# Moving a 32-block operator build from GpSimd to VectorE, and eight operator blocks of the next layer to another stage, in a two-layer SSD, GLA and S5 backbone

## The chip, the core and the metric

The kernel runs on one core of a Trainium2 chip. The metric is the device time of one execution in microseconds (us). The core has five engines that each work through their own list of instructions in order: TensorE (PE, matrix products into PSUM), VectorE (DVE), ScalarE (ACT), GpSimd (POOL) and SyncE (SP), which in this kernel issues every DMA.

## The reference, cut to what matters

A hidden stream `h` of 1024 channels by 768 tokens (256 context tokens, then 512 latent ones) passes through two layers. A layer is

```
u = rmsnorm(h) * (1 + scale) + shift
p = u @ in_proj                                  # z, x, B, C, dt | q, k, v, gates | S5 input and gate
y_ssd = ssd(...)   y_gla = gla(...)   y_s5 = s5(...)    # each in both directions, context first
h = h + gate * (concat(y_ssd * norm, y_gla, y_s5) @ out_proj)
```

The S5 branch is a linear recurrence `h_t = lam_bar * h_{t-1} + bu_t` with a complex diagonal `lam_bar`, a complex input matrix B and an output matrix C, for 32 groups of 16 channels with 64 states. The kernel does it in chunks of 8 tokens. For that it builds, per layer, from the powers of `lam_bar`:

- input operators: powers times B, in 8 blocks of 128x1024 (`s5_in_map`); they bring the 8 tokens of a chunk to the chunk's state;
- output operators: powers times C, in 16 blocks of two groups (`s5_out_map`); they bring a chunk's starting state to its 8 outputs, and with a small matrix product they give the part inside the chunk.

None of them depends on the tokens.

## The kernel before

All matrix operands are split into a high and a low part, and each product is three passes (`PASSES`): high by high, low by high, high by low. The input projection, the S5, GLA and SSD branches, their norms and the output projection are written one after another in `layer(l, u)`. A tile framework's scheduler then sorts the instructions of each engine by its own timeline of the whole program, so the order on an engine is not that of the text. SBUF tiles come from pools with tags: "cs" has 3 buffers of 128x1024, "bc" 2, "cv" 3, "bA" and "bB" one large buffer each (128x6144), "m" is one more, and "hl" has 8 for split operands. Who wants a buffer waits until its last reader is done.

The steps that the prediction speaks of:

- `s5_lambda(l)` makes the powers of `lam_bar` (tile `pw`) and writes the operands of the input operators to DRAM (`lpD`). For layer 1 it also runs in layer 0, since the ACT tables and inputs are there.
- `s5_in_map(l, bi)`, L351 to L363: loads `bb` (256 KB, L353) and `lp` (512 KB, L354), then six DVE instructions of 128x512: two products at L360, two at L361, a sum or difference at L363, twice over. The blocks of layer 0 stay in SBUF (`bls`, in bB and bA). Those of layer 1 are built in layer 0, in bA ahead of the projection of the S5 inputs, stored to `blD` (L580, 512 KB each) and loaded again in layer 1 (L602, two buffers in turn).
- `s5_out_map(l, bi, pw, buf)`, L365 to L404: loads `cb` (L370); GpSimd negates a 128x32 piece (L375) and makes the two halves of the operator in six instructions of 128x288 (L380 to L385); the result goes to DRAM (`clD`, L388); 16 small matrix products (L394) make the part inside the chunk from it, ACT copies it (L121), VectorE corrects its diagonal (L400, L401), and it goes to DRAM (`gD`). Both layers' calls run in layer 0, 16 ahead of the S5 scan and 16 behind it.
- L608 applies the input operators; L643 to L646 are the scan over chunks on VectorE; L688 and L689 apply the output operators.
- SSD ends with the sums at L928 (into `xy`); L968 multiplies by the gate, which comes from `zD`; L974, L981 and L438 make the norm, and L421 splits the normed tiles to bA and bB. The S5 outputs pass a gated unit (L1026, L1037, L1039) and are split at L421 to "hl", as are the GLA outputs that are loaded from `ygD` (L1047).
- `spilled_part` is the first half of the output projection: eight column blocks of matrix products (L1062, L1064) over the S5 and GLA operands in "hl", each added to `h` by VectorE (L1075, L1076) and stored (`hpD`). The second half takes the SSD operands in bA and bB.

```
yss = ssd_norm(0) + ssd_norm(1)
spilled_part(h1D if last else hT, 8, [a[:, :, t0:NT] for a in ygl + ys5], (4, 5, 6, 7, 0, 1, 2, 3))
```

`dma` is `nc.sync.dma_start` everywhere, so one queue holds all loads and stores in the scheduler's order. Where an entry waits for a buffer or a result, the entries behind it wait too.

Of the kernel before, what the change touches and what calls it, by code (L numbers as in the profile page):

```python
# [41 lines left out]
def hybrid_backbone_kernel(  # L42
# [52 lines left out]
    def m12():  # L95
        return T("m12", [128, 3072], 1)
# [90 lines left out]
    h1D = dram([1024, LL], "h1D")  # L187
    lpD = [dram([512, 128], f"lpD{l}") for l in range(2)]
    pwD = dram([128, 704], "pwD1")
    blD = dram([8, 128, 1024], "blD1")  # L190
    clD = [dram([16, 128, 512], f"clD{l}") for l in range(2)]
# [159 lines left out]
    def s5_in_map(l, bi, lp, bb, tb, bl):  # L351
# [6 lines left out]
        for o in range(2):  # L358
# [4 lines left out]
            V.tensor_tensor(blo, blo, tb, SUB if o == 0 else ADD)  # L363

    def s5_out_map(l, bi, pw, buf):  # L365

        gs = 2 * bi
        w5, tmp, cb, cn = cuts(buf, 576, 288, 128, 32)
        gt = tmp[:, 0:240]
# [4 lines left out]
        t54 = tmp.rearrange("p (g k h) -> p g k h", g=2, k=9)  # L374
        G.tensor_scalar(cn, cb[:, 0:32], -1.0, None, MUL)  # L375
        shp = [128, 2, 9, 16]
        pr, pi = (pw[:, :, a, gs : gs + 2].rearrange("p k g -> p g k").unsqueeze(3).to_broadcast(shp) for a in range(2))
        cr, ci, cm = (x.rearrange("p (g h) -> p g h", g=2).unsqueeze(2).to_broadcast(shp)
                      for x in (cb[:, 0:32], cb[:, 32:64], cn))
        G.tensor_tensor(w54[:, 0], pr, cr, MUL)  # L380
        G.tensor_tensor(t54, pi, ci, MUL)
        G.tensor_tensor(w54[:, 0], w54[:, 0], t54, SUB)  # L382
        G.tensor_tensor(w54[:, 1], pi, cm, MUL)
        G.tensor_tensor(t54, pr, ci, MUL)
        G.tensor_tensor(w54[:, 1], w54[:, 1], t54, SUB)  # L385
        for d in range(2):
# [89 lines left out]
    def layer(l, u):  # L476
# [93 lines left out]

        wa = wa0 if not last else big("bA")
        if not last:
            sv, wk, lt, tw, tu, pwl = cuts(wa, 480, 512, 512, 576, 576, 704)
            s5_lambda(1, sv, wk, lt, tw, tu, pwl[:, 0:576], pwl[:, 576:704])
            dma(pwD, pwl)
            for bi in range(8):
                lp = wa[:, 1024 * (bi % 2) : 1024 * (bi % 2) + 1024]
                bb, tb, bl = cuts(wa[:, 2048:4096], 512, 512, 1024)
                s5_in_map(1, bi, lp, bb, tb, bl)
                dma(blD[bi], bl)  # L580
        for i in range(4):
# [16 lines left out]
        for bi in range(16):  # L598
            if bi % 2 == 0:
                blt = bls[bi // 2] if not last else wa[:, 4096 + 1024 * (bi // 2 % 2) : 5120 + 1024 * (bi // 2 % 2)]  # L600
                if last:
                    dma(blt, blD[bi // 2])  # L602
            bl = blt.rearrange("p (a g x) -> p a g x", a=2, g=4)[:, :, 2 * (bi % 2) : 2 * (bi % 2) + 2, :]
            pst = (px, ps)[bi % 2](384)
            for gg in range(2):
                for a in range(2):
                    o = (gg * 2 + a) * 96
                    PE.matmul(pst[:, o : o + 96], bl[:, a, gg, :], ug(2 * bi + gg), start=True, stop=True)  # L608
            pv = pst.rearrange("p (g r i) -> p i r g", g=2, r=2)
            gsl = slice(2 * bi, 2 * bi + 2)  # L610
            act(st[0:64, :, :, gsl], pv[0:64], AF.Copy)
            V.tensor_copy(st[64:128, 0:32, :, gsl], pv[64:128, 31::-1])
            V.tensor_copy(st[64:128, 32:96, :, gsl], pv[64:128, 95:31:-1])
# [52 lines left out]
        hn = hn.rearrange("p r c g -> p r g c")  # L666
        if not last:
            pw1 = T("s5p", [128, 576], 1)
            dma(pw1, pwD[:, 0:576])
        c0 = 32 if last else 0  # L670
# [406 lines left out]

        def spilled_part(src, k0, rhs, order):
            for m in range(8):
                p_c, p_l = out_part(m, k0, rhs, order)  # L1080
                ho = cv(NT)
                dma(ho[:, t0:NT], src[128 * m : 128 * m + 128])
                residual(ho, ho, m, p_c, p_l)
                dma(hpD[l][128 * m : 128 * m + 128, t0:NT], ho[:, t0:NT])

        yss = ssd_norm(0) + ssd_norm(1)
# [11 lines left out]
        for m in range(8):  # L1098
# [13 lines left out]
            if m == 6:  # L1112

                act(ho[:, 0:1] if last else T("l8", [128, 128], 1)[:, 0:1], acc[:, 0:1], AF.Ln, scale=0.0, bias=1.0)
        return hx2, (acc, sq)
# [34 lines left out]
    t = [bct(), bct()]  # L1150
    wa0, wb0 = big("bA"), big("bB")
    bls = [wb0[:, 1024 * i : 1024 * i + 1024] for i in range(6)] + [wa0[:, 4096 + 1024 * i : 5120 + 1024 * i] for i in range(2)]
    lps, bbs = [a[:, 0:1024] for a in t], [a[:, 1024:1536] for a in t]
    for bi in range(8):
        s5_in_map(0, bi, lps[bi % 2], bbs[bi % 2], wa0[:, 3360:3872], bls[bi])
    hx, acc = layer(0, u)
# [7 lines left out]
    rsqrt_rows(nrm[:, 0:NT])  # L1164
    u = norm_in(1, hx, nrm)
    hx, acc = layer(1, u)
    pr = pa()
# [92 lines left out]
```

## Time and profile before

| | |
|---|---|
| median of 3 runs | 1699.73 us (1698.31 to 1706.64) |
| profiled execution | 1712.97 us |
| its span, first to last instruction | 1711.3 us, mean granted TensorE clock 0.901 |
| PE busy | 1418.1 us, 83% |
| VectorE busy | 1168.2 us, 68% |
| GpSimd busy | 783.2 us, 46% |
| ScalarE busy | 679.9 us, 40% |
| moved by DMA | 243.55 MB, 142 GB/s over the span |

The profile is of one execution, which was 13.2 us longer than the median. Busy time is the time in which an engine had an instruction running; a stretch of the program can be held by an engine that is idle half of the span elsewhere. So the shares of the span say little, and the stages are looked at one by one. In layer 0 they are: input operators and the first projections (to about 300 us), the S5 scan and the first outputs (to 465), the second set of output operators with GLA and the convolution (to 700), SSD (to 868), the norms (to 885), and the output projection (to 1022). Layer 1 runs its S5 scan from 1119 to 1230 us and ends at 1711.

### The profile page before, as it was taken

What the parts mean: (1) busy time and instruction counts of PE and PEld (TensorE: products, weight loads), DVE (VectorE), ACT (ScalarE), POOL (GpSimd) and SP (SyncE); (2) the same over time, 40 slices, a digit from 0 to 9 for tenths busy, and PEclk for the clock granted to TensorE, in tenths of its full rate; (3) what the DMA queues carried; (4) which work ended last, traced back from release to release, by engine and by line L of the source; (5) the groups of instructions that cost most, each with busy time, mean ns of one, the idle gap of its engine ahead of it and who ended that gap; (6) DMA issues with size and microseconds to landing.
All of it is one profiled execution on the core that took longest, in us unless ns stands there. A gap on an engine that the chain in (4) does not pass through costs nothing.

```text
span 1711.3 us, 23539 instructions
## 1 busy us (share of the span) xinstructions
PE 1418.1 (83%) x8536; PEld 1145.2 (67%) x8536; DVE 1168.2 (68%) x1992; ACT 679.9 (40%) x1220; POOL 783.2 (46%) x716
## 2 busy tenths in 40 slices
PE   3867766888989779977779999997889989967886
PEld 2656655777966557755668786886678777745665
DVE  7977558995477567679994127289835986688752
ACT  4312223225342336646553124343345345545442
POOL 3615647632268843445463141164123323656454
PEclk9788987898988889988889999998988999988998
DMA  8474654332543354444455745522363242344542
GB/s 308 124 185 135 178 150 135 93 118 71 176 123 86 100 165 140 142 154 139 128 187 188 282 135 178 189 85 80 111 193 107 64 139 93 119 138 145 184 131 96
DMA packets 139885, 243.55 MB, mean 142 GB/s; under 512 B 31992, under 2 KB 72568, under 8 KB 139768
## 3 DMA queue, kind: packets, MB, share of 16 engines
q1 hardware_dynamic: 139768, 242.04, 45.3%
q8 instruction: 67, 1.10, 0.3%
q14 instruction: 50, 0.41, 0.1%
HBM read 192.81 MB, written 49.18 MB: 141 GB/s over the span
## 4 chain that ended last, share of the span: by engine, by line
PE 25%; DVE 18%; DMA 13%; POOL 6%; issue 4%; ACT 4%; SPq 0%; DVEq 0%; ACTq 0%; POOLq 0%
PE pl L492 7%; PE pl L1062 6%; DMA bA<-acsD 5%; DMA bB<-acsD 3%; PE pc L494 2%; PE pc L1064 2%; DVE xy L863 1%; DMA wr<-in_wblk 1%; ACT bA L121 1%; POOL wl L416 1%; DVE bB L916 1%; DVE bA L916 1%; DVE xy L645 1%; DMA cs<-zD 1%; DVE bA L644 1%
## 5 line engine op out<-in xcount | busy, mean ns | idle before, releaser
L492 PE MATMUL pl<-hl,wh 128*128 128x512 f32 (+1 forms) x1184 | 411.5, 414 | 15.9 <-DVE ev L511 12.3
L416 POOL TENSOR_TENSOR wl<-wr,wh 128x1024 fp32r<-128x1024 f32 (+1 forms) x82 | 210.4, 2566 | 308.5 <-ACT wh L121 284.6
L492 PEld LDWEIGHTS pl<-hl,wh 128*128 128x128 f32 (+1 forms) x1184 | 226.0, 195 | 73.5 <-DVE ev L511 13.6
L492 PE MATMUL pl<-hl,wl 128*128 128x512 f32 (+1 forms) x592 | 243.5, 412 | 20.0 <-POOL wl L416 10.7
L121 ACT ACTIVATE wh<-wr 128x1024 fp32r<-128x1024 f32 (+1 forms) x122 | 127.6, 1047 | 283.7 <-PE pc L1064 69.3
L494 PE MATMUL pc<-hl,wh 128*128 128x256 f32 (+1 forms) x864 | 202.0, 304 | 11.3 <-DVE ev L511 7.2
L494 PEld LDWEIGHTS pc<-hl,wh 128*128 128x128 f32 (+1 forms) x864 | 152.5, 202 | 26.1 <-DVE ev L511 8.7
L492 PEld LDWEIGHTS pl<-hl,wl 128*128 128x128 f32 (+1 forms) x592 | 115.4, 195 | 49.1 <-POOL wl L416 12.0
L494 PE MATMUL pc<-hl,wl 128*128 128x256 f32 (+1 forms) x432 | 128.6, 298 | 0.0
L1062 PE MATMUL pl<-hl,wh 128*128 128x512 f32 x256 | 87.7, 419 | 16.9 <-ACT hl L121 4.6
L394 PE MATMUL pa<-cs 64*32 64x128 f32 x512 | 42.9, 305 | 64.0 <-POOL cs L382 27.3
L494 PEld LDWEIGHTS pc<-hl,wl 128*128 128x128 f32 (+1 forms) x432 | 87.3, 202 | 2.7 <-issue 1.7
L121 ACT ACTIVATE ev<-pl 128x512 f32<-128x512 f32 (+1 forms) x96 | 51.1, 534 | 87.7 <-PE pl L709 43.9
L709 PE MATMUL pl<-wh,hl 128*128 128x256 f32 x384 | 79.6, 307 | 2.6 <-ACT ev L121 2.6
L416 DVE TENSOR_TENSOR wl<-wr,wh 128x1024 fp32r<-128x1024 f32 x40 | 55.4, 1386 | 38.3 <-ACT wh L121 38.1
L121 ACT ACTIVATE bB<-bB 128x512 f32<-128x512 f32 (+4 forms) x40 | 45.7, 1142 | 85.1 <-DMA bB<-acsD 52.3
L394 PEld LDWEIGHTS pa<-cs 64*32 64x32 f32 x512 | 21.5, 115 | 80.6 <-POOL cs L382 28.9
L863 DVE SCALAR_TENSOR_TENSOR xy<-ev,par_sb,xy 128x512 f32<-128x512 f32 (+1 forms) x112 | 74.8, 704 | 0.6
L375 POOL TENSOR_SCALAR cs<-cs 128x32 f32<-128x32 f32 x32 | 20.1, 629 | 118.4 <-DMA cs<-in_s5cb 43.3
L709 PEld LDWEIGHTS pl<-wh,hl 128*128 128x128 f32 x384 | 66.9, 214 | 7.8 <-ACT ev L121 3.8
L1062 PEld LDWEIGHTS pl<-hl,wh 128*128 128x128 f32 x256 | 49.8, 199 | 31.1 <-ACT hl L121 6.7
L709 PE MATMUL pl<-wl,hl 128*128 128x256 f32 x192 | 58.4, 308 | 3.8 <-DVE wl L416 3.8
(483 smaller groups left out, 3604.4 us busy)
## 6 DMA issues: line engine op xcount, KB each, us to landing
wr<-in_wblk SPq DMA_DIRECT2D x80, 512.0 KB
wr<-in_wout SPq DMA_DIRECT2D x32, 512.0 KB
hl<-in_mod_w SPq DMA_DIRECT2D x20, 512.0 KB
bA<-acsD SPq DMA_DIRECT2D x10, 1024.0 KB
bB<-acsD SPq DMA_DIRECT2D x10, 1024.0 KB
clD<-cs SPq DMA_DIRECT2D x64, 128.0 KB
cs<-clD SPq DMA_DIRECT2D x32, 256.0 KB
cs<-in_mod_w SPq DMA_DIRECT2D x16, 512.0 KB
```

The costliest lines, as they stand in the source:

```text
L121: return S.activation(out, in_, f, **kw)
L375: G.tensor_scalar(cn, cb[:, 0:32], -1.0, None, MUL)
L394: PE.matmul(pk[d][32 * gg : 32 * gg + 32], b0[64 * d : 64 * d + 64, a, :], w54[64 * d : 64 * d + 64, a, gg, d : 8 + d, :].rearrange("p k h ...
L416: (eng or (V if wcount[0] % 3 == 0 else G)).tensor_tensor(wl, wr, wh.bitcast(F32), SUB)
L492: PE.matmul(p_l[:m], lhs, u[k][:, ui, LC:NT], start=st, stop=sp)
L494: PE.matmul(p_c[:m], lhs, u[k][:, ui, 0:LC], start=st, stop=sp)
L644: V.tensor_tensor(tr[:, 1, :n], li, src[:, :, ::-1], MUL)
L709: PE.matmul(p, u[k][:, ui, 128 * c : 128 * c + 128], ws[k // 4][wi][:, 256 * (k % 4) : 256 * (k % 4) + 256], start=n == 0, stop=n == 23)
L863: V.scalar_tensor_tensor(ac, raw[:, o + k : o + k + n], pcol("cw", w0 + k), ac, MUL, ADD)
L916: V.scalar_tensor_tensor(rf[:, h, :], rbw[:, h, :], rb[:, ih : ih + 1], rf[:, h, :], SUB, MIN)
L1062: PE.matmul(p_l, lhs, rhs[kk][:, ui, LC - t0 : NT - t0], start=st, stop=sp)
L1064: PE.matmul(p_c, lhs, rhs[kk][:, ui, 0:LC], start=st, stop=sp)
```

## The change

Five edits. (1) `s5_out_map` builds its operator with six VectorE instructions of 128x288 in place of seven GpSimd ones; the negation is folded into the last one. (2) The eight `s5_in_map` calls of layer 1 move from ahead of the projection of the S5 inputs to `spilled_part` of layer 0, one behind each column block; they load into the two "bc" tiles and build in the "m" tile. (3) In layer 1 all eight blocks are loaded at once into places in bB (six) and bA (two), behind the norm, where before they came in turn through two buffers. (4) `s5_lambda(1)` and layer 0's blocks get other places in bA. (5) The reload of layer 1's powers stands behind the y5 loop. A table load of ACT is written into another tile.

```
+    def s5_in_home():
+
+        wa, wb = big("bA"), big("bB")
+        return wa, [wb[:, 1024 * i : 1024 * i + 1024] for i in range(6)] + [wa[:, 1024 * i : 1024 * i + 1024] for i in range(2)]
+
     def s5_out_map(l, bi, pw, buf):
...
-        G.tensor_scalar(cn, cb[:, 0:32], -1.0, None, MUL)
...
-        G.tensor_tensor(w54[:, 0], pr, cr, MUL)
-        G.tensor_tensor(t54, pi, ci, MUL)
-        G.tensor_tensor(w54[:, 0], w54[:, 0], t54, SUB)
-        G.tensor_tensor(w54[:, 1], pi, cm, MUL)
-        G.tensor_tensor(t54, pr, ci, MUL)
-        G.tensor_tensor(w54[:, 1], w54[:, 1], t54, SUB)
...
+        V.tensor_tensor(w54[:, 0], pr, cr, MUL)
+        V.tensor_tensor(t54, pi, ci, MUL)
+        V.tensor_tensor(w54[:, 0], w54[:, 0], t54, SUB)
+        V.tensor_tensor(w54[:, 1], pi, cr, MUL)
+        V.tensor_tensor(t54, pr, ci, MUL)
+        V.scalar_tensor_tensor(w5[:, 288:576], w5[:, 288:576], -1.0, tmp, MUL, SUB)
...
             s5_lambda(1, sv, wk, lt, tw, tu, pwl[:, 0:576], pwl[:, 576:704])
             dma(pwD, pwl)
-            for bi in range(8):
-                lp = wa[:, 1024 * (bi % 2) : 1024 * (bi % 2) + 1024]
-                bb, tb, bl = cuts(wa[:, 2048:4096], 512, 512, 1024)
-                s5_in_map(1, bi, lp, bb, tb, bl)
-                dma(blD[bi], bl)
...
         for bi in range(16):
-            if bi % 2 == 0:
-                blt = bls[bi // 2] if not last else wa[:, 4096 + 1024 * (bi // 2 % 2) : 5120 + 1024 * (bi // 2 % 2)]
-                if last:
-                    dma(blt, blD[bi // 2])
...
         def spilled_part(src, k0, rhs, order):
+            if not last:
+                t, wm = [bct(), bct()], m12()
             for m in range(8):
...
                 dma(hpD[l][128 * m : 128 * m + 128, t0:NT], ho[:, t0:NT])
+                if not last:
+
+                    bl = wm[:, 1024 * (m % 2) : 1024 * (m % 2) + 1024]
+                    s5_in_map(1, m, t[m % 2][:, 0:1024], t[m % 2][:, 1024:1536], wm[:, 2048:2560], bl)
+                    dma(blD[m], bl)
...
     u = norm_in(1, hx, nrm)
+    _, bls = s5_in_home()
+    for bi in range(8):
+        dma(bls[bi], blD[bi])
     hx, acc = layer(1, u)
```

The text of the change does not show where the scheduler puts the pieces. The rows below are the built order of one engine. Line numbers in the rows of the changed kernel are its own: its L961, L967, L974, L1030, L1032, L425 and L1068 are L968, L974, L981, L1037, L1039, L421 and L1075 of before, and L921 is L928.

VectorE before, from the last sum of SSD (L928) to the last split of a GLA operand that the output projection needs (L421 to "hl"):

```order
L928 TENSOR_TENSOR xy_4123<-xy_4123,ps_6054 128x4x128
L421 TENSOR_TENSOR hl_6842<-cv_6840,hl_6842 128x768
L421 TENSOR_TENSOR hl_6847<-cv_6845,hl_6847 128x768
L968 TENSOR_TENSOR xy_4123<-xy_4123,cs_6870 128x768
L968 TENSOR_TENSOR xy_4123<-xy_4123,cs_6875 128x768
L421 TENSOR_TENSOR hl_6852<-cv_6850,hl_6852 128x768
L438 TENSOR_TENSOR ev_6863<-ev_6863,cs_6875 128x768
L421 TENSOR_TENSOR hl_6857<-cv_6855,hl_6857 128x768
```

The same place in the changed kernel holds 54 instructions between the last sum of SSD and the last of these splits; its end is this, with "m" the tile of the input operators of layer 1 (L360, L361 and L363) and bA and bB the operands of the second half:

```order
L361 TENSOR_TENSOR m_674_6842<-bc_6841 128x512
L974 SCALAR_TENSOR_TENSOR xy_4019<-xy_4019,par_sb,ev_6818 128x768 x4
L425 TENSOR_TENSOR hl_6738<-cv_6736,hl_6738 128x768
L363 TENSOR_TENSOR m_674_6842<-m_674_6842 128x512
L425 TENSOR_TENSOR hl_6743<-cv_6741,hl_6743 128x768
L425 TENSOR_TENSOR bB_6827<-xy_4019,bB_6827 128x768 x2
L361 TENSOR_TENSOR m_674_6842<-bc_6840 128x512
L425 TENSOR_TENSOR hl_6748<-cv_6746,hl_6748 128x768
L425 TENSOR_TENSOR hl_6753<-cv_6751,hl_6753 128x768
L360 TENSOR_TENSOR m_674_6842<-bc_6841 128x512 x2
L363 TENSOR_TENSOR m_674_6842<-m_674_6842 128x512
L1069 SCALAR_TENSOR_TENSOR cv_6898<-pl_6849,modp,cv_6898 128x512
```

What moved: the four splits to "hl" stood right behind SSD, and now the whole norm of both halves, two gated units and 21 instructions of the input operators stand ahead of the last of them and of the first addition to `h` (L1069, before L1076).

SP's queue before, at the loads of the GLA outputs (cv from ygD) that these splits read:

```order
L1047 DMA cv_6840<-ygD_125 128x768
L1047 DMA cv_6845<-ygD_125 128x768
L412 DMA wr_7124<-in_wout 128x1024
L966 DMA cs_6870<-zD_107 128x768
L966 DMA cs_6875<-zD_107 128x768
L1047 DMA cv_6850<-ygD_125 128x768
L1047 DMA cv_6855<-ygD_125 128x768
```

And SP's queue in the changed kernel at the same loads (L1040 there), with the stores of finished blocks (blD from m) and the loads of later ones (bc from in_s5b and lpD):

```order
L1084 DMA blD_132<-m_674_6842 128x1024
L231 DMA cs_8004<-in_mod_w 128x1024
L1040 DMA cv_6736<-ygD_125 128x768
L353 DMA bc_6840<-in_s5b 128x1x512
L354 DMA bc_6840<-lpD_131 128x1x1024
L231 DMA cs_8010<-in_mod_w 128x1024
L416 DMA wr_7050<-in_wout 128x1024
L1084 DMA blD_132<-m_674_6842 128x1024
L231 DMA cs_8016<-in_mod_w 128x1024
L1040 DMA cv_6741<-ygD_125 128x768
L353 DMA bc_6841<-in_s5b 128x1x512
L354 DMA bc_6841<-lpD_131 128x1x1024
```

What moved: stores that wait for VectorE and loads that wait for "bc" now stand between the four loads, which followed one another closely before.

In the early part VectorE's rows of one output operator (cs, L384 to L389 of the changed kernel) now stand between the small instructions of `s5_lambda(1)` (bA):

```order
L384 TENSOR_TENSOR cs_1186<-s5p_139,cs_1186 128x288
L385 TENSOR_TENSOR cs_1186<-s5p_139,cs_1186 128x288
L387 TENSOR_TENSOR cs_1186<-s5p_139,cs_1186 128x288
L348 TENSOR_TENSOR bA_484<-bA_484 64x9x32
L349 TENSOR_TENSOR bA_484<-bA_484 64x9x32
```

Before, only rows of `s5_lambda(1)` stood there, and the operators were GpSimd's:

```order
L345 TENSOR_TENSOR bA_484<-bA_484 128x576
L346 TENSOR_TENSOR bA_484<-bA_484 128x576
L348 TENSOR_TENSOR bA_484<-bA_484 64x9x32
L349 TENSOR_TENSOR bA_484<-bA_484 64x9x32
L348 TENSOR_TENSOR bA_484<-bA_484 64x9x32
```

## Rows read from the trace of the kernel before

**Rows 1.** Stages: start:end, length, busy PE, PEld, DVE, ACT, POOL, clock, DMA share, GB/s.

```profile
50.00:300.00 250.00, 184.68 (x1173) 150.53 (x1173) 176.31 (x328) 61.71 (x122) 131.10 (x130) 0.84 0.56 153
...
465.00:650.00 185.00, 149.93 (x1030) 116.39 (x1028) 123.38 (x208) 59.56 (x122) 128.65 (x164) 0.88 0.44 127
...
700.00:868.00 168.00, 128.25 (x737) 99.31 (x736) 151.19 (x252) 91.23 (x225) 87.71 (x62) 0.86 0.45 144
...
885.00:1022.00 137.00, 134.99 (x831) 111.26 (x832) 46.27 (x55) 37.54 (x43) 50.10 (x22) 0.99 0.57 204
...
1084.00:1119.00 35.00, 35.00 (x234) 31.77 (x233) 11.27 (x33) 13.35 (x24) 5.66 (x7) 1.00 0.56 181
1119.00:1230.00 111.00, 92.39 (x537) 78.06 (x537) 109.14 (x148) 37.43 (x53) 51.63 (x39) 0.91 0.31 97
```

**Rows 2.** Waits of PE from 50 to 300 us: us, times, longest.

```profile
PE pa L394 <- POOL cs L382: 27.0, 6, 9.4
PE pa L394 <- DVE cs L400: 12.9, 6, 5.3
```

**Rows 3.** Waits of PE from 300 to 650 us.

```profile
PE pa L394 <- ACT cs L121: 18.7, 3, 11.8
```

**Rows 4.** Groups of GpSimd: count, busy us, mean ns, idle before.

```profile
L380 POOL TENSOR_TENSOR cs<-s5p,cs 128x288 f32<-128x288 f32 x32 | 34.7, 1084 | 0.0
...
L384 POOL TENSOR_TENSOR cs<-s5p,cs 128x288 f32<-128x288 f32 x32 | 27.3, 857 | 0.9
...
L375 POOL TENSOR_SCALAR cs<-cs 128x32 f32<-128x32 f32 x32 | 20.1, 629 | 118.4 <-DMA cs<-in_s5cb 43.3 <-DVE bA L361 18.8 <-DMA clD<-cs 16.1
```

**Rows 5.** Waits of VectorE from 50 to 300 us.

```profile
DVE bA L360 <- DMA blD<-bA: 15.6, 4, 7.0
DVE bA L361 <- DMA bA<-in_s5b: 15.5, 5, 4.5
...
DVE bA L360 <- DMA bA<-lpD: 8.1, 1, 8.1
```

**Rows 6.** Groups of VectorE, shapes kept apart.

```profile
L361 DVE TENSOR_TENSOR bA<-bA 128x512 f32<-128x512 f32 x16 | 18.2, 1135 | 25.8 <-DMA bA<-in_s5b 15.5 <-issue 10.2
L363 DVE TENSOR_TENSOR bA<-bA 128x512 f32<-128x512 f32 x20 | 14.3, 713 | 0.2
L360 DVE TENSOR_TENSOR bA<-bA 128x512 f32<-128x512 f32 x16 | 12.1, 789 | 23.7 <-DMA blD<-bA 15.6 <-DMA bA<-lpD 8.1
L361 DVE TENSOR_TENSOR bA<-bc 128x512 f32<-128x512 f32 x16 | 11.8, 737 | 0.0
...
L360 DVE TENSOR_TENSOR bA<-bc 128x512 f32<-128x512 f32 x4 | 2.6, 687 | 7.8 <-DMA bc<-lpD 7.8
...
L348 DVE TENSOR_TENSOR s5p<-cs,cs 64x288 f32<-64x288 f32 x2 | 0.9, 450 | 0.0
```

**Rows 7.** VectorE in order of time from 62 us: start, us, instruction.

```profile
65.44 0.18 DVE L251 SCALAR_TENSOR_TENSOR bA<-bA 128x32 f32<-128x32 f32 x1
...
66.16 0.77 DVE L251 SCALAR_TENSOR_TENSOR bA<-bA 128x32 f32<-128x32 f32 x1
```

**Rows 8.** VectorE in order of time from 860 to 900 us.

```profile
860.26 1.53 DVE L1037 SCALAR_TENSOR_TENSOR cv<-cv,cv 128x768 f32<-128x768 f32 x1
...
867.93 0.67 DVE L928 TENSOR_TENSOR xy<-xy,ps 128x512 f32<-128x512 f32 x1
...
873.37 1.81 DVE L968 TENSOR_TENSOR xy<-xy,cs 128x768 f32<-128x768 f32 x2
...
878.83 0.94 DVE L421 TENSOR_TENSOR hl<-cv,hl 128x768 fp32r<-128x768 f32 x1
...
885.08 0.75 DVE L1076 SCALAR_TENSOR_TENSOR cv<-pl,modp,cv 128x512 f32<-128x512 f32 x1
...
890.45 5.94 DVE L981 SCALAR_TENSOR_TENSOR xy<-xy,par_sb,ev 128x768 f32<-128x768 f32 x4
...
898.82 2.56 DVE L421 TENSOR_TENSOR bA<-xy,bA 128x768 fp32r<-128x768 f32 x1
```

More of the change, by code (lines that the diff above doesn't have):

```diff
@@ L188, in hybrid_backbone_kernel @@
     lpD = [dram([512, 128], f"lpD{l}") for l in range(2)]
+    blD = dram([8, 128, 1024], "blD1")
     pwD = dram([128, 704], "pwD1")
-    blD = dram([8, 128, 1024], "blD1")
     clD = [dram([16, 128, 512], f"clD{l}") for l in range(2)]
@@ L363, in s5_in_map @@
             V.tensor_tensor(blo, blo, tb, SUB if o == 0 else ADD)
+    def s5_in_home():
+        wa, wb = big("bA"), big("bB")
+        return wa, [wb[:, 1024 * i : 1024 * i + 1024] for i in range(6)] + [wa[:, 1024 * i : 1024 * i + 1024] for i in range(2)]
     def s5_out_map(l, bi, pw, buf):
         gs = 2 * bi
-        w5, tmp, cb, cn = cuts(buf, 576, 288, 128, 32)
+        w5, tmp, cb = cuts(buf, 576, 288, 128)
         gt = tmp[:, 0:240]
@@ L374, in s5_out_map @@
         t54 = tmp.rearrange("p (g k h) -> p g k h", g=2, k=9)
-        G.tensor_scalar(cn, cb[:, 0:32], -1.0, None, MUL)
         shp = [128, 2, 9, 16]
         pr, pi = (pw[:, :, a, gs : gs + 2].rearrange("p k g -> p g k").unsqueeze(3).to_broadcast(shp) for a in range(2))
-        cr, ci, cm = (x.rearrange("p (g h) -> p g h", g=2).unsqueeze(2).to_broadcast(shp)
-                      for x in (cb[:, 0:32], cb[:, 32:64], cn))
-        G.tensor_tensor(w54[:, 0], pr, cr, MUL)
-        G.tensor_tensor(t54, pi, ci, MUL)
-        G.tensor_tensor(w54[:, 0], w54[:, 0], t54, SUB)
-        G.tensor_tensor(w54[:, 1], pi, cm, MUL)
-        G.tensor_tensor(t54, pr, ci, MUL)
-        G.tensor_tensor(w54[:, 1], w54[:, 1], t54, SUB)
+        cr, ci = (x.rearrange("p (g h) -> p g h", g=2).unsqueeze(2).to_broadcast(shp)
+                  for x in (cb[:, 0:32], cb[:, 32:64]))
+        V.tensor_tensor(w54[:, 0], pr, cr, MUL)
[4 more added lines that the diff above has]
+        V.scalar_tensor_tensor(w5[:, 288:576], w5[:, 288:576], -1.0, tmp, MUL, SUB)
         for d in range(2):
@@ L568, in layer @@
             dma(acsD[l][:, d].rearrange("c h l -> h c l"), rows.rearrange("h (c l) -> h c l", c=6))
-        wa = wa0 if not last else big("bA")
         if not last:
-            sv, wk, lt, tw, tu, pwl = cuts(wa, 480, 512, 512, 576, 576, 704)
+            sv, wk, lt, tw, tu, pwl = cuts(wa0[:, 2560:], 480, 512, 512, 576, 576, 704)
             s5_lambda(1, sv, wk, lt, tw, tu, pwl[:, 0:576], pwl[:, 576:704])
             dma(pwD, pwl)
-            for bi in range(8):
-                lp = wa[:, 1024 * (bi % 2) : 1024 * (bi % 2) + 1024]
-                bb, tb, bl = cuts(wa[:, 2048:4096], 512, 512, 1024)
-                s5_in_map(1, bi, lp, bb, tb, bl)
-                dma(blD[bi], bl)
         for i in range(4):
@@ L598, in layer @@
         for bi in range(16):
-            if bi % 2 == 0:
-                blt = bls[bi // 2] if not last else wa[:, 4096 + 1024 * (bi // 2 % 2) : 5120 + 1024 * (bi // 2 % 2)]
-                if last:
-                    dma(blt, blD[bi // 2])
-            bl = blt.rearrange("p (a g x) -> p a g x", a=2, g=4)[:, :, 2 * (bi % 2) : 2 * (bi % 2) + 2, :]
+            bl = bls[bi // 2].rearrange("p (a g x) -> p a g x", a=2, g=4)[:, :, 2 * (bi % 2) : 2 * (bi % 2) + 2, :]
             pst = (px, ps)[bi % 2](384)
@@ L666, in layer @@
         hn = hn.rearrange("p r c g -> p r g c")
-        if not last:
-            pw1 = T("s5p", [128, 576], 1)
-            dma(pw1, pwD[:, 0:576])
         c0 = 32 if last else 0
@@ L694, in layer @@
         if not last:
+            pw1 = T("s5p", [128, 576], 1)
+            dma(pw1, pwD[:, 0:576])
             for bi in range(16):
@@ L1112, in layer @@
             if m == 6:
-                act(ho[:, 0:1] if last else T("l8", [128, 128], 1)[:, 0:1], acc[:, 0:1], AF.Ln, scale=0.0, bias=1.0)
+                act(ho[:, 0:1], acc[:, 0:1], AF.Ln, scale=0.0, bias=1.0)
         return hx2, (acc, sq)
@@ L1150, in hybrid_backbone_kernel @@
     t = [bct(), bct()]
-    wa0, wb0 = big("bA"), big("bB")
-    bls = [wb0[:, 1024 * i : 1024 * i + 1024] for i in range(6)] + [wa0[:, 4096 + 1024 * i : 5120 + 1024 * i] for i in range(2)]
-    lps, bbs = [a[:, 0:1024] for a in t], [a[:, 1024:1536] for a in t]
+    wa0, bls = s5_in_home()
     for bi in range(8):
-        s5_in_map(0, bi, lps[bi % 2], bbs[bi % 2], wa0[:, 3360:3872], bls[bi])
+        s5_in_map(0, bi, t[bi % 2][:, 0:1024], t[bi % 2][:, 1024:1536], wa0[:, 2048:2560], bls[bi])
     hx, acc = layer(0, u)
```

## The prediction

> **What bounds the kernel now.** I read the stages first [rows 1], then what PE waits for in those that the change touches [rows 2, 3], then the groups of GpSimd and VectorE [rows 4, 6] and VectorE's own waits [rows 5], and last VectorE instruction by instruction where SSD hands over to the output projection [rows 8]. No engine bounds the whole. From 50 to 300 us PE has 184.68 us of work in 250 and VectorE 176.31: both idle for a quarter or more, so waits set this stage. From 465 to 650 PE has 149.93 of 185 and VectorE 123.38. SSD, 700 to 868, is VectorE's: 151.19 of 168. The output projection, 885 to 1022, is PE's: 134.99 of 137, with VectorE at 46.27. In layer 1 the 35 us ahead of the S5 scan are PE's (35.00), the scan to 1230 is VectorE's (109.14 of 111) [rows 1].
>
> Inside the two stages with the output operators, PE's largest waits stand in front of their small products L394: 27.0 us for GpSimd's part and 12.9 for VectorE's diagonal correction in the first, 18.7 in the second for ACT, which stands at the end of an earlier block's chain in the same three buffers [rows 2, 3]. That is 58.6 us. VectorE meanwhile waits 15.6 + 15.5 + 8.1 = 39.2 us for the DMAs of the second layer's input operators [rows 5], which share SP's queue with the loads and stores of the output operators; GpSimd's first step of a block waits 43.3 us for its load [rows 4].
>
> **The change, part by part.** *Output operators, work.* A block costs GpSimd 0.63 us and six instructions between 0.857 and 1.084 [rows 4], some 6.5 us together; 32 blocks hold it about 207 us. For VectorE's 128x288 there is no row. The nearest has the same 288 elements a partition on 64 partitions, 0.450 us; above it lies 0.687 at 512 elements [rows 6]. I take 0.45, so 2.7 us a block, 43 us for 16 blocks and 86 us for all 192 instructions. A block's chain gets some 3.8 us shorter.
>
> *First stage.* VectorE gets 43 us and loses the input operators of layer 1: 18.2 + 12.1 + 16 of the 20 at 0.713 = 41.7 us [rows 6]. Its work stays at about 177 of 250 us; it is its 39.2 us of waits, and the queue entries behind them, that go. PE's idle time there is 65 us [rows 1], 39.9 of it in front of L394 [rows 2]. I take 85% of these waits, 34 us, since the chain is less than half as long in its operator part and its loads are no longer queued behind 24 transfers. The bounds are 5 us, if the small products wait for VectorE as they did for GpSimd, and 65, if all of PE's idle time closes.
>
> *Second stage.* VectorE would have 123.38 + 43 = 166 us of work in 185. So this stage can give up at most 19 us before VectorE is full, and 18.7 us of wait are to be had [rows 3]. I take 12, between 0 and 19. SSD and the convolution hold no output operators and move as a whole. Gain to the end of SSD: 46 us.
>
> *SSD to output projection.* Before, six VectorE instructions stand between the last sum of SSD at 867.93 and the last split to "hl" at 878.83, and the first addition to h comes at 885.08 [rows 8]. In the changed order there are 54. What is new among them: 21 instructions of input operators at 0.687, 0.737 and 0.713 [rows 6], 15.0 us; four more L968 at half of 1.81, 3.6; eight L981 at 5.94/4, 11.9; four splits to bA and bB between 0.94 and 2.56, say 7.0; two L1037 at 1.53, 3.1; nine small ones (L1039, L974, L438) priced as the 0.67 of L928, 6.0 [rows 8]. Together 46.6 us. Two of the gated units among them (two L1037, four L1039, 5.8 us) stood ahead of L928 before, where VectorE was full, so the last sum comes that much earlier. Loss: 41 us. The projection can't start its columns in earnest before these splits, its operand; and what VectorE has done early is not given back, since the projection is PE's and VectorE has 90 us to spare in it. Bounds: 15, if the norm's part is covered by a wait that is there anyway and only the input operators count, and 50 if their slower price of 1.135 for L361 [rows 6] returns.
>
> *SP's queue at the same place.* 24 more transfers (8 times 768 KB in and 512 KB out) stand between the loads of gate and GLA operands. Each store waits for VectorE and each pair of loads for a "bc" tile. At their old place such transfers held VectorE for 39.2 us [rows 5]; here there are twelve or more VectorE instructions between a block's end and the next use of its tile. I take 6 us, between 0 and 39.
>
> *Layer 1.* All reloads come ahead, so L608 is no longer paced by two buffers. PE is full in the 35 us before the scan, so nothing is gained there as such; but in the built order some 20 us of projection work move from ahead of the last L608 to behind it, and the scan holds 111 - 92.4 = 18.6 us of PE idle time to take them [rows 1]. VectorE gets the GLA preparation, which stood ahead, into the scan. I take 8 us gained, between -3 and 18. The other places in bA, the reload of the powers and the ACT table are covered by PE's work in the y5 loop and cost a DMA of about 2 us if that cover goes; I count nothing.
>
> **Sum.** 1712.97 - 46 + 41 + 6 - 8 = 1706 us for the profiled execution. That execution lies 13.2 us above the median of the runs, so 1693 us against 1699.7. The likeliest result is thus a gain upstream that is nearly all handed back at the norms: its own range is 1680 to 1708.
>
> **Rivals.** *The blocks are hidden.* VectorE has 90 us free in the projection [rows 1]; if the norm stage costs only the input operators' 15 us, the sum is 1712.97 - 46 + 15 + 0 - 8 - 13.2 = 1661; with the upper 65 + 19 ahead, 1623. Against it: VectorE does these instructions in order, ahead of splits that PE needs. I put it at 1660, chance 0.18.
>
> *VectorE was the victim.* The same 128x32 instruction takes 0.18 us and, beside a GpSimd operator, 0.77 [rows 7]; 0.6 us each on up to 224 meetings would be 130 us of VectorE time, of which I guess a fifth, 25 us, falls where VectorE sets the pace. Then it is 1668. In the sum this is left at nothing, since most meetings fall where VectorE has time. Chance 0.08. The Trainium skill, "SBUF — State Buffer", section on SBUF's two separate sides, says that a VectorE instruction with two SBUF inputs and a GpSimd instruction take a shared port in turn, one blocked for the whole of the other; by that rule each meeting costs a whole GpSimd instruction, which the pair of rows agrees with, and the time would be the one of this rival.
>
> *SP's queue stalls the projection* (the other side). If the 24 transfers hold the GLA loads as they held VectorE before, 39 us in place of 6, it is 1726. It decides from 15 us above my 6 on: then the change is slower than no change can be told. For it speaks that three of the four ygD loads stand behind stores that wait for VectorE; against it, that the loads into "bc" have no reader for some 10 us. Chance 0.17.
>
> *VectorE takes GpSimd's place.* PE waits in front of L394 as long as before, now for VectorE, which does operators between 177 us of other work. The gain ahead is 5 + 10 in place of 46, the time 1724. Chance 0.13.
>
> *It does nothing measurable*, since the scheduler's other order evens out: within the first case.
>
> **How the numbers follow.** Forecast 0.44. Half a per cent, 8.5 us, is about what a measurement of this kernel can tell from no change. Faster (below 1691.2): the two fast rivals with 0.26 and four tenths of the forecast, 0.18: 0.44. Slower (above 1708.2): the two slow rivals but for their mild ends, 0.26, and 0.03 of the forecast: 0.29. Same: 0.27. The range is 1655 to 1727: it reaches to the fast rivals' middle and to the slow ones', and leaves out about a tenth on each side.
>
> **What would show it.** Right: PE's wait in front of L394 falls from 58.6 to under 20 us; the S5 scan, which now starts just ahead of 300 us, starts before 260; the last L928 comes at about 820; from there to the first L1076 (L1069 in the new numbering) some 55 to 60 us pass, with VectorE near full and PE idle, where it was 17; the projection lasts 137 us as before. Wrong: L394 waits for VectorE's operators by 30 us or more; or the gap at the norms is under 30 us; or VectorE itself waits there for zD, bc or ygD by more than 20 us; or the scan of layer 1 starts later behind the end of layer 0 than the 97 us of before. The S5 prices are wrong if the 128x288 instructions come out over 0.6 us.

## The result and the profile after

The changed kernel takes 1724.08 us (median, 1721.38 to 1728.8), against 1702.87 for the kernel before in the same series: a ratio of 1.0129, 95% interval 1.0091 to 1.0167. The forecast was 1693, with a range to 1727: the time lies inside it, on the other side of the kernel before. The profiled execution took 1728.8 us, its span is 1727.0.

The page of the changed kernel, busy time by engine:

```profile
PE 1435.7 (83%) x8536; PEld 1157.4 (67%) x8536; DVE 1190.9 (69%) x2184; ACT 676.8 (39%) x1216; POOL 593.1 (34%) x492
```

GpSimd has lost 190 us and VectorE has gained 23. In the kernel before the shares of the span looked as if VectorE had room; here they still do, and the kernel is slower.

The stages of the changed kernel, with the columns of [rows 1]:

```profile
50.00:212.00 162.00, 139.55 (x932) 109.26 (x930) 125.14 (x352) 42.73 (x98) 19.53 (x10) 0.94 0.55 145
...
815.00:879.00 64.00, 36.67 (x128) 26.05 (x128) 62.57 (x60) 30.20 (x35) 26.01 (x11) 0.71 0.68 192
879.00:1017.00 138.00, 134.81 (x841) 110.90 (x844) 39.20 (x57) 23.83 (x28) 33.98 (x16) 0.99 0.64 218
...
1099.00:1211.00 112.00, 93.76 (x526) 80.28 (x525) 103.80 (x137) 36.66 (x51) 51.16 (x36) 0.89 0.27 87
1211.00:1293.00 82.00, 74.12 (x421) 66.16 (x419) 20.96 (x50) 32.92 (x30) 15.12 (x14) 0.73 0.52 155
```

The first stage of [rows 1] ended at 300 us; the S5 scan now starts at 213. From there on the kernel is read best by its milestones. All are starts of VectorE instructions, in us, in the trace of one execution of each kernel. "First addition" and "last addition" are those of layer 0's output projection to h; the scan of layer 1 is given behind the last addition, and the last column is the span's end minus the last addition. Five kernels below have the same layer 0 (changed, e1, e5, e8, e11) and end it between 1009.8 and 1019.5 us, so a difference of a few us in one milestone says little.

| kernel | S5 scan | last SSD sum | first addition to h | last addition | then scan of layer 1 | layer 1 |
|---|---|---|---|---|---|---|
| before | 291 | 868 | 885.1 | 1022.3 | +96.7 | 689.0 |
| changed | 213 | 815 | 878.6 | 1016.5 | +82.1 | 710.5 |

In these two executions layer 0 got 5.8 us shorter and layer 1 21.5 us longer. PE's waits from 50 to 650 us, which answer to [rows 2, 3], with L398 in L394's place:

```profile
PE pa L398 <- DVE cs L386: 7.6, 2, 6.7
...
PE pa L398 <- issue: 5.8, 5, 2.1
...
PE pa L398 <- DVE cs L389: 1.7, 2, 1.4
```

58.6 us of waits in front of the small products are down to 15.1. The groups of VectorE that make the operators now, which answer to [rows 4, 6]:

```profile
L384 DVE TENSOR_TENSOR cs<-s5p,cs 128x288 f32<-128x288 f32 x32 | 25.1, 785 | 25.4 <-DMA cs<-in_s5cb 25.1 <-issue 0.3
...
L389 DVE SCALAR_TENSOR_TENSOR cs<-cs 128x288 f32<-128x288 f32 x32 | 15.0, 471 | 0.3
...
L385 DVE TENSOR_TENSOR cs<-s5p,cs 128x288 f32<-128x288 f32 x32 | 14.4, 449 | 0.0
```

Five of the six cost 0.447 to 0.473 us, as priced; the first one, which stands behind the block's load, has 0.785 on the mean. All 192 together are 98 us, forecast 86.

At the norms, VectorE from 814 us in order of time, which answers to [rows 8]:

```profile
814.67 0.68 DVE L921 TENSOR_TENSOR xy<-xy,ps 128x512 f32<-128x512 f32 x1
...
819.94 2.74 DVE L361 TENSOR_TENSOR m<-bc 128x512 f32<-128x512 f32 x1
...
840.42 7.50 DVE L974 SCALAR_TENSOR_TENSOR xy<-xy,par_sb,ev 128x768 f32<-128x768 f32 x4
...
861.34 7.36 DVE L974 SCALAR_TENSOR_TENSOR xy<-xy,par_sb,ev 128x768 f32<-128x768 f32 x4 [0.95 <-ACT ev L121]
...
874.95 1.81 DVE L425 TENSOR_TENSOR hl<-cv,hl 128x768 fp32r<-128x768 f32 x2
876.69 1.28 DVE L360 TENSOR_TENSOR m<-bc 128x512 f32<-128x512 f32 x2
877.89 0.68 DVE L363 TENSOR_TENSOR m<-m 128x512 f32<-128x512 f32 x1
878.60 0.75 DVE L1069 SCALAR_TENSOR_TENSOR cv<-pl,modp,cv 128x512 f32<-128x512 f32 x1
```

From the last SSD sum to the first addition 64 us pass, where it was 17. The row of 815 to 879 above shows what that is: VectorE works 62.57 of 64 us, some 22 of them in 24 instructions of the input operators ("m"). PE works 36.67, and its mean granted clock is 0.71 of full speed (2.4 GHz).

In layer 1 the trace shows a wait for q and k that the kernel before didn't have. VectorE's waits from 1100 to 1500 us, two of the longest:

```profile
DVE ev L515 <- ACT ev L121: 38.0, 8, 10.2
...
DVE bB L750 <- DMA bB<-qkD: 23.4, 1, 23.4
```

The second is one wait of 23.4 us, at the load of q and k for the second half of the GLA heads. In the kernel before, VectorE's longest wait at the same line (L757 there) is for ACT, and shorter:

```profile
DVE cv L757 <- ACT cv L121: 14.4, 1, 14.4
```

SP's queue in that stretch: start, us, the line and the transfer that it issued.

```profile
1212.07 6.44 SPq L743 DMA_DIRECT2D bB<-qkD  x2
1229.13 0.33 SPq L670 DMA_DIRECT2D cs<-clD  x1
...
1246.94 0.32 SPq L670 DMA_DIRECT2D cs<-clD  x1
1247.31 1.21 SPq L673 DMA_DIRECT2D cs<-gD  x2
1248.57 0.45 SPq L744 DMA_DIRECT2D bB<-vD  x1
1249.07 1.19 SPq L742 DMA_DIRECT2D bB<-qkD  x2
```

Between 1229 and 1247 SP issues the loads of six y5 blocks (L670, L673; a seventh went at 1210), each when a "cs" buffer is freed by a product of the y5 loop, and only then q and k. SP's rows of the other kernels with all loads on its queue show the same split. Where the blocks are loaded in turn (before, e1, e3, e4, e6, e10), these q loads stand behind one y5 block's loads. Where they come early (changed, e2, e5, e7), they stand behind seven. Only e11 and e12 load early and have one. In the stretch 1211 to 1293 VectorE is busy for 20.96 of 82 us and PE's mean granted clock is 0.73. The 82 us behind the scan of the kernel before:

```profile
1230.00:1312.00 82.00, 75.95 (x509) 68.45 (x511) 31.97 (x65) 44.30 (x48) 20.39 (x27) 0.83 0.54 160
```

VectorE, ACT (44.30 us against 32.92) and GpSimd each did more there, and PE's clock was 0.83.

### The profile page after: what moved, and what is told of

Read it like the earlier page. It is cut to its first block, busy times and chain, and to the rows that moved or that the text cites. A ratio compares the mean times of both kernels' runs of the same rounds, so it can differ in the third digit from the quotient of the medians.

```text
span 1727.0 us, 23431 instructions
## 1 busy us (share of the span) xinstructions
PE 1435.7 (83%) x8536; PEld 1157.4 (67%) x8536; DVE 1190.9 (69%) x2184; ACT 676.8 (39%) x1216; POOL 593.1 (34%) x492
## 5 line engine op out<-in xcount | busy, mean ns | idle before, releaser
L496 PE MATMUL pl<-hl,wh 128*128 128x512 f32 (+1 forms) x1184 | 414.3, 417 | 16.9 <-ACT ev L121 8.7
L1055 PE MATMUL pl<-hl,wh 128*128 128x512 f32 x256 | 92.3, 435 | 24.9 <-ACT cv L121 10.5
L1019 PE MATMUL pl<-hl,wh 128*128 128x512 f32 x128 | 52.8, 486 | 19.0 <-ACT cv L121 18.6
L702 PE MATMUL pl<-wl,hl 128*128 128x256 f32 x192 | 58.6, 308 | 11.2 <-POOL wl L420 11.2
L1055 PE MATMUL pl<-hl,wl 128*128 128x512 f32 x128 | 54.9, 429 | 1.8 <-POOL wl L420 1.7
L398 PE MATMUL pa<-cs 64*32 64x128 f32 x512 | 41.9, 289 | 16.3 <-DVE cs L386 7.6
```

The lines of the kernel that those rows point to most:

```text
L398: PE.matmul(pk[d][32 * gg : 32 * gg + 32], b0[64 * d : 64 * d + 64, a, :], w54[64 * d : 64 * d + 64, a, gg, d : 8 + d, :].rearrange("p k h ...
L496: PE.matmul(p_l[:m], lhs, u[k][:, ui, LC:NT], start=st, stop=sp)
L702: PE.matmul(p, u[k][:, ui, 128 * c : 128 * c + 128], ws[k // 4][wi][:, 256 * (k % 4) : 256 * (k % 4) + 256], start=n == 0, stop=n == 23)
L1019: PE.matmul(p_l, lhs, yg5[k][:, ui, LC:NT], start=n == 0, stop=n == 11)
L1055: PE.matmul(p_l, lhs, rhs[kk][:, ui, LC - t0 : NT - t0], start=st, stop=sp)
```

## The experiments

Each row is a kernel of its own, timed against the kernel before on the same chip; milestones as above.

| run | median us | ratio to before, 95% | last SSD sum | first addition | last addition | scan of layer 1 | layer 1 |
|---|---|---|---|---|---|---|---|
| e1 | 1702.3 | 0.9979 (0.9954 to 1.0005) | 814 | 878.5 | 1015.8 | +96.7 | 687.4 |
| e2 | 1723.95 | 1.0113 (1.0074 to 1.0152) | 866 | 882.6 | 1019.9 | +81.4 | 705.8 |
| e3 | 1709.06 | 1.0021 (1.0001 to 1.0042) | 883 | 884.6 | 1027.1 | +96.5 | 683.2 |
| e4 | 1720.24 | 1.0106 (1.0068 to 1.0143) | 844 | 892.5 | 1036.7 | +96.7 | 689.7 |
| e5 | 1720.13 | 1.0098 (1.0067 to 1.0129) | 818 | 881.9 | 1019.5 | +81.7 | 706.0 |
| e6 | 1693.02 | 0.9939 (0.9916 to 0.9963) | 798 | 852.6 | 999.6 | +96.7 | 685.1 |
| e7 | 1713.09 | 1.0045 (1.0022 to 1.0069) | 807 | 863.5 | 1007.5 | +81.7 | 707.1 |
| e8 | 1723.69 | 1.0098 (1.0063 to 1.0133) | 809 | 872.5 | 1009.8 | +81.5 | 699.7 |
| e9 | 1712.85 | 1.0040 (1.0011 to 1.0069) | 805 | 861.1 | 1008.1 | +96.7 | 704.3 |
| e10 | 1716.34 | 1.0061 (1.0030 to 1.0092) | 827 | 874.2 | 1027.0 | +96.8 | 689.2 |
| e11 | 1706.34 | 1.0002 (0.9976 to 1.0029) | 815 | 879.7 | 1017.5 | +81.5 | 683.9 |
| e12 | 1689.62 | 0.9924 (0.9900 to 0.9948) | 804 | 860.0 | 1006.3 | +81.5 | 679.6 |

**e1, the reload of before in the changed kernel.**

```
+            if bi % 2 == 0:
+                blt = bls[bi // 2] if not last else wa[:, 4096 + 1024 * (bi // 2 % 2) : 5120 + 1024 * (bi // 2 % 2)]
+                if last:
+                    dma(blt, blD[bi // 2])
...
-    _, bls = s5_in_home()
-    for bi in range(8):
-        dma(bls[bi], blD[bi])
```

> The changed kernel with one edit undone: layer 1 again loads the eight input operator blocks in turn through two buffers in bA, where the changed kernel loads all at once into bB and bA. Theory 1: layer 0 of the changed kernel is no slower (it ends 5 us earlier), and the 21 us are lost in layer 1, because the blocks sit in bB and push the GLA work that needs bB behind them. Then layer 1 takes about 689 us again, as before, and the time is about 1703. Theory 2: the 21 us come from the later place of the input operators, and layer 1 is only shifted; then it stays above 1718.

1702.3, layer 1 at 687.4 us. With the reload of before, the rest of the change is worth 2 us, which can't be told from nothing.

**e2, the new reload in the kernel before**, the same edit the other way round.

```
-            if bi % 2 == 0:
-                blt = bls[bi // 2] if not last else wa[:, 4096 + 1024 * (bi // 2 % 2) : 5120 + 1024 * (bi // 2 % 2)]
...
+    wa1, wb1 = big("bA"), big("bB")
+    bls = [wb1[:, 1024 * i : 1024 * i + 1024] for i in range(6)] + [wa1[:, 1024 * i : 1024 * i + 1024] for i in range(2)]
+    for bi in range(8):
+        dma(bls[bi], blD[bi])
     hx, acc = layer(1, u)
```

> The kernel before with one edit alone: layer 1 loads all eight blocks at once into bB and bA. Theory 1: layer 1 gets about 20 us longer, the time is about 1722. Theory 2: within 8 us of 1703.

1723.95, layer 1 at 705.8 us, and layer 0 as before. So the whole of what can be measured of this change is the edit that loads all blocks at once. It was one of the two small terms of the prediction's sum, and the only one forecast as a gain in layer 1.

**e3, only the output operators on VectorE.** The function `s5_out_map` of the changed kernel in the kernel before.

```
-        G.tensor_scalar(cn, cb[:, 0:32], -1.0, None, MUL)
...
-        G.tensor_tensor(w54[:, 0], pr, cr, MUL)
+        V.tensor_tensor(w54[:, 0], pr, cr, MUL)
...
```

> The kernel before with the output operators on VectorE alone; the input operators of layer 1 stay at their old place. Theory 1 (the norms give back what this wins, and without the input operators there they don't): some 30 us won ahead of SSD and no 47 us lost at the norms, so 1665 to 1685. Rival (VectorE takes GpSimd's place, and the win ahead came from the input operators' leaving): 1695 or more.

1709.06: the rival was right in the time, but the waits did not stay. PE's largest waits in front of the small products (L393 here), from 50 to 650 us:

```profile
PE pa L393 <- DVE cs L399: 8.9, 3, 6.8
PE pa L393 <- DVE cs L384: 4.4, 6, 1.4
PE pa L393 <- DVE cs L381: 3.6, 2, 2.6
```

That is 16.9 us, where the largest three before were 58.6, and still nothing is gained. The scan starts at 277 us in place of 291, but its last step starts at 406 in both: it got 14 us longer. In the rows of these stretches, of the kernel before

```profile
291.00:402.00 111.00, 96.87 (x602) 81.73 (x603) 102.74 (x169) 25.54 (x44) 58.34 (x55) 0.94 0.34 105
```

and of e3

```profile
277.00:402.00 125.00, 90.53 (x510) 75.94 (x508) 111.90 (x173) 24.08 (x39) 57.66 (x52) 0.82 0.26 77
```

PE does less inside the scan than before (90.53 us at a clock of 0.82, where it was 96.87 at 0.94), since it had done more ahead of it: from the start to 402 us both kernels have run some 1940 products. What is won ahead of the scan is given back inside it. The last SSD sum comes 15 us later than before, but other work has moved ahead of it: the first addition to h comes when it came before (884.6 against 885.1).

**e4, only the place of the input operators.** e1 with the `s5_out_map` of before.

```
-        V.tensor_tensor(w54[:, 0], pr, cr, MUL)
+        G.tensor_tensor(w54[:, 0], pr, cr, MUL)
...
```

> The kernel before with the input operators of layer 1 built at the output projection alone; output operators on GpSimd, reload through two buffers. Theory 1: their 39 us of waits ahead go, worth some 20 us at the end of SSD, and the norms take 15 to 47 us longer, so 1700 to 1730. Rival (the place costs nothing, VectorE has room in the projection): 1680 to 1690.

1720.24: the last SSD sum comes 24 us earlier, the first addition to h 7 us later, and the projection takes 144 us where it took 137. The expectation's range held, and its rival is out. The 24 us come although the three largest waits in front of the small products are still 42.2 us (19.6, 12.7 and 9.9).

**e5, six blocks at once, but in bA.** Is it bB, which GLA needs, that costs the time in layer 1? Against e1:

```
-                blt = bls[bi // 2] if not last else wa[:, 4096 + 1024 * (bi // 2 % 2) : 5120 + 1024 * (bi // 2 % 2)]
+                blt = bls[bi // 2] if not last else wa[:, 1024 * (bi // 2 % 6) : 1024 * (bi // 2 % 6) + 1024]
```

> As e1 (output operators on VectorE, input operators at the output projection), but layer 1 loads six of its eight blocks at once into bA and the last two into the first two's places; bB stays free for GLA, which it was not in the changed kernel. Theory 1a (the 21 us in layer 1 come from bB being taken): about 1702 or, with the scan 10 us earlier, 1690 to 1702. Theory 1b (they come from applying all blocks early, with the projection work put off into the scan): 1715 or more.

1720.13, layer 1 at 706.0 us: bB isn't it. What e2, e5 and the changed kernel share is the scan of layer 1 that starts 15 us earlier behind layer 0.

**e6, the input operators tied behind their column block.** Written behind the block, the scheduler had pulled them ahead of all of them.

```
+                    V.tensor_copy(bl[:, 0:1], ho[:, NT - 1 : NT])
+                    V.tensor_copy(bl[:, 512:513], ho[:, NT - 1 : NT])
+                    V.tensor_copy(wm[:, 2048:2049], ho[:, NT - 1 : NT])
                     s5_in_map(1, m, t[m % 2][:, 0:1024], t[m % 2][:, 1024:1536], wm[:, 2048:2560], bl)
```

> As e1, but each input operator block of layer 1 is tied behind the addition to h of its own column block, by three one-column VectorE copies out of that tile into the block's tiles, so that VectorE can't do it ahead of the splits. If the input operators hold the splits at the norms, the 64 us from the last SSD sum to the first addition fall by the 15 us of their 21 instructions or more, and the time is 1680 to 1692 with e1 at 1702. If VectorE has that time anyway (the norm's own rows or the loads set the gap), it stays within 5 us of 1702.

1693.02, 9 us less than e1. The traced execution ends layer 0 16 us earlier than e1's, but it was 6 us faster than its median; over all kernels with these layers 0, the four tied ones (e6, e7, e9, e12) end it at 1005.4 us on the mean and the five untied ones (changed, e1, e5, e8, e11) at 1015.8. So the tie is worth some 10 us. The way there was not the one expected. Between the last SSD sum and the first addition 24 instructions are gone, some 22 us, but the gap shrinks by 10 only (55 us in place of 64; the norm's own rows still stand ahead of the splits), and the projection, with the operators now in it, gives these back (147 us in place of 137). What is left at the end of layer 0 is there already at the last SSD sum (803.7 on the mean of the tied, 814.0 of the untied). Six operator instructions, some 5 us, stood ahead of that sum in e1; where the other 5 us come from is not shown.

**e7, e5 and e6 together:** e6 with the places of e5.

```
+                blt = bls[bi // 2] if not last else wa[:, 1024 * (bi // 2 % 6) : 1024 * (bi // 2 % 6) + 1024]
```

> e5 and e6 together. If both effects are independent, the time is e1 plus the differences of e5 and e6 to it; by theory 1a and 15 us at the norms that is 1675 to 1690.

1713.09. The differences add up within the scatter (1702.3 + 17.8 - 9.3 = 1710.8), the expectation by theory 1a doesn't hold.

**e8, the late loads off SP's queue.**

```
+            dq = nc.gpsimd.dma_start if last and hd > 1 else dma
             for rs in (lo_, hi_):
-                dma(q[rs, t0:NT], qkD[l][64 * hd : 64 * hd + 64, t0:NT])
+                dq(q[rs, t0:NT], qkD[l][64 * hd : 64 * hd + 64, t0:NT])
```

and so for k and v.

> The changed kernel, with the q, k and v loads of the last two GLA heads of layer 1 issued by GpSimd in place of SP. In the changed kernel VectorE waits 23.4 us in one piece for these q and k at 1254 us; SP issues them at 1249, behind the loads of seven y5 blocks that each wait for a cs buffer. If SP's order is what loses the time in layer 1, the wait falls under 13 us (bB is free at about 1237) and the time by some 10 us, to 1708 to 1716. If the wait is for PE's or ACT's work, GpSimd waits as long, and the time stays within 5 us of 1724.

The time is 1723.69: the prediction for the time failed. Its executions scatter more than others (1711 to 1731), and the profiled one is the fastest, so its layer 1 of 699.7 us stands for the lower end. The wait fell, but not as far as it should, and the next one took its place. VectorE's waits of e8 from 1100 to 1350 us:

```profile
DVE bB L751 <- DMA bB<-qkD: 15.2, 1, 15.2
DVE cv L751 <- ACT cv L121: 11.0, 1, 11.0
```

The second is the wait for ACT that the kernel before had too. GpSimd issued the q and k loads at 1233 us, 16 us earlier than SP had:

```profile
1233.32 1.04 POOL L743 DMA_DIRECT2D bB<-qkD  x2 [8.38 <-PE ps L805]
```

That is 142 us behind the start of the scan; in the changed kernel it was some 150, in the kernel before 123. GpSimd too had to wait, for the last products of GLA's first half (L805), which read bB and which y5 also stands ahead of. So the queue is one place where the time shows, not its cause.

**e9, the same loads off SP's queue in e6.**

```
+            dq = nc.gpsimd.dma_start if last and hd > 1 else dma
```

> e6 with the same loads on GpSimd. There they were issued with one y5 block's loads ahead, so by the theory of SP's order little is to be had: 1687 to 1695. Rival: any load off SP's queue helps as much, so 1680 to 1686.

1712.85, 20 us slower than e6, with layer 1 at 704.3 us. Neither the expectation nor its rival. VectorE's longest wait from 1100 to 1350 us is

```profile
DVE cv L756 <- ACT cv L121: 24.8, 1, 24.8
```

where e6 has 14.5 at the same line. While VectorE waits, ACT takes out three results of y5, from 1265 to 1280 us, each after waiting for PE, before the copy that VectorE needs; in e6 it takes out two. So y5 stands further ahead of GLA here too, without an early scan. That this is the whole of the 20 us is not shown.

**e10, e6 with GpSimd's output operators.**

```
-        V.tensor_tensor(w54[:, 0], pr, cr, MUL)
+        G.tensor_tensor(w54[:, 0], pr, cr, MUL)
...
```

> e6 with the output operators back on GpSimd. If VectorE's building of them is worth what e1 against e4 shows (18 us) it is 1708 to 1714. Rival: that difference came from the places of the input operators, which are now tied; then it is within 5 us of 1693.

1716.34. With the input operators out of the way, VectorE's building is worth 23 us (e10 to e6; 21 by the ratios, since the two were timed in different series). In the kernel before it is worth nothing (e3). The two edits need each other. How much of the 23 us is the shorter chain and how much other VectorE instructions getting faster (last section) was not separated.

**e11, the y5 loop of layer 1 written behind GLA.**

```
         if not last:
             mod_tiles(0, 16, 8)
+        else:
+            y5_loop()
```

with the loop as it was in `y5_loop`, called at its old place in layer 0.

> The changed kernel, with the y5 loop of layer 1 (products with the output operators) written behind the GLA heads in place of ahead of them, so that the scheduler gives GLA's second half the way: its q and k loads stand behind one y5 block's loads in SP's queue, not seven. Theory: what layer 1 loses (710 us from the last addition of layer 0 to the end, against 687 in e1) is that y5 runs ahead of GLA's second half and leaves VectorE idle; then layer 1 takes 690 us or less and the time is 1695 to 1706. Rival (the early scan delays the input projection, whatever follows): layer 1 stays over 700 us and the time over 1714.

1706.34, layer 1 at 683.9 us, 26.6 less than in the changed kernel and level with e1 (687.4). The scan starts as early as there (+81.5). VectorE's wait for q and k in e11:

```profile
DVE bB L753 <- DMA bB<-qkD: 5.7, 1, 5.7
```

and the row of the stretch behind the scan, to be held against those of the changed kernel and of the kernel before above:

```profile
1211.00:1293.00 82.00, 75.86 (x542) 67.01 (x541) 33.45 (x76) 45.12 (x47) 24.53 (x26) 0.92 0.57 163
```

VectorE, ACT and GpSimd each do more in the same 82 us than in the changed kernel, and PE's clock is 0.92 in place of 0.73. How much of the difference is the waits and how much the clock was not separated.

**e12, e7 with the y5 loop behind GLA,** by the edit of e11.

```
+        else:
+            y5_loop()
```

> e7 (input operators tied behind their column block, six blocks loaded at once into bA) with the y5 loop of layer 1 behind GLA. If the theory of e11 holds, layer 1 falls from e7's 708 us to 690 or less, and the time from 1713 to 1690 to 1696; if the early scan is worth something once y5 is out of the way, to 1680. Rival: 1707 to 1716.

1689.62, layer 1 at 679.6 us, a little better than expected: the lowest median here, 0.8% ahead of the kernel before. Its interval overlaps with that of e6, which has no early scan, and e11's with that of e1. So with y5 out of the way the early scan costs nothing, and gains nothing that these runs can tell.

## Why the prediction was wrong

Its layer 0 held in the numbers, though not in every account of them, and the signs that it named for layer 0 came but for PE, which is not idle at the norms (36.67 of 64 us).

- Output operators: 98 us in all against 86. Five of six instructions took 0.447 to 0.473 us against 0.45; the first took 0.785, above the 0.6 that was to show the prices wrong. L394's waits are 15 us where "under 20" was to show it right; the scan starts at 213 us, "before 260".
- Gain to the end of SSD: 46 forecast, 53 measured (868 to 815). The sum came out in part by luck, since its account did not hold: I had 34 us of it from PE's waits in front of L394, which the shorter chain and the freed queue together would remove. In e3 these waits go with the shorter chain alone, and the first addition to h comes no earlier. In e4 42.2 us of them stay, and the input operators' leaving alone brings the last SSD sum 24 us forward. Only both give 53.
- Norms: 41 us and 6 for SP's queue forecast, 47 measured (64 - 17). VectorE waits 1.4 of the 64 us, so the 6 us for SP's queue are not there; they were VectorE's own work. Of the 47, e6 takes back 10 by taking the input operators out, and the projection gives these back. The rest, the norm's own rows ahead of the splits, was only argued from the order: no run put them back.
- Layer 0 as a whole: +1 us forecast, -5.8 measured, a difference that lies within the scatter of the milestones.

The step that failed is **"Layer 1": "I take 8 us gained, between -3 and 18"**. It lost 21.5 us, outside its own bounds. Half of the mechanism that it names is there: the scan starts 14.6 us earlier behind layer 0 (+82.1 in place of +96.7), and +81.4 to +82.1 in every run that loads the blocks early. The other half is not: PE's idle time in the scan was to take up the projection work that was put off, but PE works 93.76 of 112 us there (row of 1099 to 1211), where it was 92.39 of 111 [rows 1]. And the step ended at the scan. Behind it the scheduler had put the y5 loop of layer 1 ahead of GLA's second half. y5 is small products whose loads each wait for a buffer; while it runs, GLA's second half waits for q and k, VectorE is busy for 20.96 of 82 us where it was 31.97, and PE's mean granted clock is 0.73 where it was 0.83. e2 and e1 show that the edit alone costs the time, e5 that bB has no part in it, e11 and e12 that the order of y5 and GLA takes it and gives it back. That it is SP's queue alone fell with e8. Why the scheduler ranks the two so was not looked into.

The slower rivals had times of 1724 and 1726, which the kernel met by chance: as mechanisms they were wrong. L394 waits 15 us, and SP's queue doesn't hold the projection: between the last SSD sum and the first addition VectorE works 62.57 of 64 us. Nor is *VectorE takes GpSimd's place* borne out by e3, where the waits went and the time stayed.

## What to carry to other kernels

An edit that lets a stage start earlier is not costed at that stage's start: read in the built order what the early start lets go ahead of what, down to the next stage that all engines share. A place in the text is only a wish where a scheduler sorts by readiness, so independent work that must not go ahead needs a data dependency (e6), and a stage that should yield can be written behind the other, if the built order then follows (e11). A wait that is gone is not yet time won: e3 removed most of the waits in front of the small products, and gained nothing. Two edits of which neither wins alone can win together (e3 and e10 against e6), so an edit that was measured alone and dropped may be worth another run once its neighbour has changed.

## What the runs showed of the hardware

One instruction of VectorE, L251 with 128x32 elements on bA, was 358 ns on the mean in the kernel with GpSimd's operators and is 174 ns without them; first the kernel before, then the changed one:

```profile
L251 DVE SCALAR_TENSOR_TENSOR bA<-bA 128x32 f32<-128x32 f32 x12 | 4.3, 358 | 0.0
```

```profile
L251 DVE SCALAR_TENSOR_TENSOR bA<-bA 128x32 f32<-128x32 f32 x12 | 2.1, 174 | 0.0
```

The mean hides two kinds. Four of the twelve took 0.69 to 0.77 us, all between 66 and 73 us, where GpSimd worked through the operators without a gap. The other eight took 0.18 or 0.19, and two of these ran inside the record of a GpSimd instruction (one at 108.22 us, beside an L416 of 4.50 us that began at 107.03). The Trainium skill, "SBUF — State Buffer", section on SBUF's two separate sides, says that a VectorE instruction with two SBUF inputs and a GpSimd instruction that reads SBUF contend for a port, which the one that starts first holds for its whole length while the other is blocked. The four long rows agree with it; the two short ones show that VectorE is not blocked every time that a GpSimd instruction is on record.

From e10 to e6, which differ in the operators' engine alone, VectorE gets 192 instructions more, 103 us by their durations, and its busy time grows by 31.7 us (1165.8 to 1197.5). Most of the rest is other instructions getting shorter: over the groups that stand in both kernels in equal number, 1855 instructions, the durations sum to 1238 us in e10 and to 1188 in e6. From the kernel before to e3 such groups lose 57 us in the same way. The prediction gave this relief a chance of 0.08 and left it out of the sum. It is there, but in e3, where it comes with the operators on VectorE alone, no time is gained.
